# A hybrid mixer layer on one core: recurrence levels as one run of ten products, gate modulation in runs of two blocks

## The chip, the cores and the metric

The kernel runs on one core of one Trainium2 chip. The time is the device time of one execution in microseconds (us). Before the change the median of three runs is 438.06 us (437.89 to 438.6). The profile is of one more execution, which took 439.14 us.

## The reference

One layer of a diffusion backbone. 128 context tokens and 512 latent tokens of width 1024 (640 rows in all) are normalised and modulated, go through one input projection, then through three parallel mixers (attention, a gated linear recurrence in two directions, a Fourier mixing), each times a SiLU gate, and through one output projection. A second normalisation, a modulation gate and a residual add end it. Cut to what the change touches:

```python
mod = silu(c) @ w_ada + b_ada              # one vector for the context, one for the latent tokens
shift, scale, gate = split(mod, 3)         # 1024 each
h = rmsnorm(x, g_pre) * (1 + scale) + shift
proj = h @ w_in
...
# recurrence, per head (64 keys x 64 values), forward and backward over the tokens:
#   state_t = f_t * state_{t-1} + k_t v_t ,  out_t = q_t state_t
...
out = concat(attention * silu(ga), rms(recurrence) * silu(gr), fourier * silu(gf)) @ w_out
x = x + gate * rmsnorm(out, g_post)
```

The change touches two places: the recurrence inside chunks of 128 tokens, and the products silu(c) @ w_ada, in particular those for `gate`.

## The kernel before

The 640 rows lie transposed in SBUF (`hT`, a high and a low part, so that three products of the reduced type fp32r stand for one fp32 product). The input projection goes in 30 blocks of 128 columns. For each block `load_raw` (L172) brings 512 KB of weights into a tile tagged `raw`; `split_w` makes a high part by a copy on ScalarE (L127) and a low part by a subtraction on VectorE (L128), in tiles `hi` and `lo` of three buffers each; then 48 products of 320 columns follow (`block`, L295). The tag `raw` has two buffers, which the weights of the input projection (`win`), the gate (`wg`) and the output projection (`wout`) share. All weight loads go out on SyncE's queue, and `tc.issue_after(wdma[-1])` in `load_raw` keeps them in the order in which the program was written down.

That order is made by `Order` (L39): streams (generators) for the start, the recurrences of two head pairs (p = 0 and 1), the attentions, the gate vectors and the filling projection blocks are taken in turn by a rough clock of TensorE's work, and events let a stream wait for another, as `block18` for the end of the 18th projection block. The blocks are written down in the order of `FILL` (L30); blocks 18 to 26 are the second gate block of the recurrence, a gate block of attention, value, query and key of attention pair 3, two gate blocks of the Fourier mixing and its two inputs. What is written down goes through a scheduler that simulates the engines and may take a later instruction first if an earlier one isn't ready. `follow` (L115) ties a product to the one before it in a list without a semaphore, so that the two keep their order on TensorE.

**Modulation.** `mod_cols` (L192) multiplies silu of the two conditioning vectors (`csil`, 32 columns) with a block of 128 columns of w_ada, k = 0 to 7. The eight fp32 products write to four strips of 32 rows of one bank, k and k + 4 to the same strip. In `start_stream` (L242) each of eight steps does two such blocks into one bank, for scale and shift. In `gate_vectors` (L842) eight steps q each wait for `block18` to `block25`, load one block of gate weights, do one `mod_cols` into a bank of its own and split the result into two halves of `rows`; after each odd q four products with `selr` (L870) sum the strips and spread the vector over the partitions.

**Recurrence.** For each head pair p, `recurrence` (L412) builds the matrix of decayed query-key products of each 128-token unit in seven levels h = 1, 2, 4, ... 64. At each level ScalarE (L458 to L461) and VectorE (L464 to L473) prepare `QB` and `KB`. `level` (L429) then does ten fp32 products of 64 rows: five units times two heads. The heads lie in the two halves of the rows. The first eight go to two banks, the last two to two more. Then the wanted part of each bank is copied into `AL` (units 0 to 3) and `AC` (unit 4): at the first level all of it by ScalarE, at the others by `copy_predicated` on VectorE (L448) with a mask of the token pairs whose indices first differ at this level. For h = 64 that mask is the two off-diagonal quadrants of 64x64. The banks come from `PB()`, which has five buffers for its tag `b` and three for the tag `f` of the projection blocks. After the last level the diagonal is set by two more masked copies for each head (L485, L486).

Of the kernel before, what the change touches and what calls it, by code (L numbers as in the profile page):

```python
# [10 lines left out]
F32R = mybir.dt.float32r  # L11
# [6 lines left out]
P = 128  # L18
# [4 lines left out]
LEVELS = [1, 2, 4, 8, 16, 32, 64]  # L23
# [48 lines left out]
def mixer_kernel(ctx: ExitStack, tc: tile.TileContext, A, O):  # L72
    nc = tc.nc
    sc, ve, gp, te, sy = nc.scalar, nc.vector, nc.gpsimd, nc.tensor, nc.sync
# [5 lines left out]
    sp = ctx.enter_context(tc.tile_pool(name="sp", bufs=WB["s"]))  # L80
    ps = ctx.enter_context(tc.tile_pool(name="ps", bufs=8, space=PSUM))

    od = Order()
# [3 lines left out]
    def nm(s):  # L87
        n_[0] += 1
        return f"{s}_{n_[0]}"

    def T(cols=NT, dt=F32, tag=""):
        return tp.tile([P, NT], dt, tag="t", name=nm("t" + tag))[:, :cols]
# [12 lines left out]
    def PB(tag="b"):  # L105
        return ps.tile([P, 512], F32, tag=tag, name=nm("pb"), bufs=WB["p" + tag])
# [3 lines left out]
    def mm(out, lhsT, rhs, start=True, stop=True):  # L110
        n, m = rhs.free_size(), lhsT.free_size()
        od.now += 1e-3 * (n * 0.4167 * 4 if rhs.dtype == F32 else max(n * 0.4167, m * 0.83)) + 2e-3
        return te.matmul(out, lhsT, rhs, start=start, stop=stop).ins  # L113

    def follow(chain, ins):  # L115

        if chain:
            tc.add_manual_dep(ins, chain[-1].name, mybir.DependencyInfo(mybir.DependencyClass.NoSync,
                                                                        mybir.DependencyReason.DATA), reason="turns")
        chain.append(ins)  # L120
# [5 lines left out]
    def split(src, hi, lo, hi_eng=None, lo_eng=None):  # L126
        (sc.copy if hi_eng is None else hi_eng.tensor_copy)(hi, src)  # L127
        (ve if lo_eng is None else lo_eng).tensor_sub(lo, src, hi.bitcast(F32))  # L128
# [5 lines left out]
    def const(name, shape, dt=F32, dma=gp.dma_start):  # L134
        t = cp.tile([P, *shape], dt, tag=name, name=name)
        if name in A:
            dma(t, A[name])
        return t
# [6 lines left out]
    RS = [slice(0, 64), slice(64, 128)]  # L145
# [20 lines left out]
    csil = const("csil", [KT, 32])  # L166
# [5 lines left out]
    def load_raw(src, tag, shape=(KT, P)):  # L172
        t = (tp if tag == "vs" else wp).tile([P, *shape], F32, tag=tag, name=nm(tag), bufs=WB[tag])
        with tc.issue_after(wdma[-1]) if wdma else ExitStack():
            wdma.append(sy.dma_start(t, src).ins)
        return t
# [12 lines left out]
        with tc.issue_after(wdma[-1]) if wdma else ExitStack():  # L189
            sy.dma_start(t, src)  # L190

    def mod_cols(out, w):  # L192

        t = od.now
        for k in range(KT):
            o = out[32 * (k % 4):32 * (k % 4) + 32, :]
            mm(o, csil[:, k, :], w[:, k, :], start=(k < 4), stop=(k >= 4))
        od.now = t + 0.45

    shift, G, rstd = const("shift", [KT, 2]), const("G", [KT, 2]), const("rstd", [5])  # L200
# [14 lines left out]
    def load_x():  # L215
        for i in range(5):
            load(xa[i], A["x"][i * P:(i + 1) * P, 0:NT])
            load(xb[i], A["x"][i * P:(i + 1) * P, NT:D])

    def scale_x():  # L220
        for i in range(5):
            ss2 = S(2)
            sc.activation(T(), xa[i], ACT.Square, accum_out=ss2[:, 0:1])
            ve.tensor_tensor_reduce(PE_()[:, 0:384], xb[i], xb[i], 1.0, 0.0, op0=ALU.mult, op1=ALU.add,
                                    accum_out=ss2[:, 1:2])
            ve.tensor_add(rstd[:, i:i + 1], ss2[:, 0:1], ss2[:, 1:2])
            rsqrt_mean(rstd[:, i:i + 1], D)
            ve.tensor_scalar(xa[i], xa[i], rstd[:, i:i + 1], 0.0, op0=ALU.mult, op1=ALU.add)
            ve.tensor_scalar(xb[i], xb[i], rstd[:, i:i + 1], 0.0, op0=ALU.mult, op1=ALU.add)
# [12 lines left out]
    def start_stream():  # L242
        load_x()
        raws, zraw = [], []

        def loads(k):
            for u in range(2):
                raws.append(load_raw(A["wss"][2 * k + u], RAW[2 * k + u]))
            if k < 2:
                zraw.append(load_raw(A["win"][k], "raw"))  # L250

        for k in range(EARLY):
            loads(k)
        scale_x()
        od.now = 11.0
        for k in range(KT):
            if k + EARLY < KT:
                loads(k + EARLY)
            row = sp.tile([P, 256], F32, tag="AC", name=nm("row"), bufs=2)
            pm = PB()  # L260
            for u in range(2):
                mod_cols(pm[:, u * P:(u + 1) * P], raws[2 * k + u])
            yield 0
            ve.tensor_copy(row, pm[:, 0:256])
            yield LAT["row"]
            pt = pm[:, 256:260]
            for u in range(2):
                mm(pt[:, u * 2:u * 2 + 2], row[:, u * P:(u + 1) * P], sel[:, :, 0:1].rearrange("p a b -> p (a b)"))
            ve.tensor_scalar(G[:, k, :], pt[:, 0:2], bss[:, k, 0:1], 1.0, op0=ALU.add, op1=ALU.add)
            ve.tensor_scalar_mul(G[:, k, :], G[:, k, :], gpre[:, k:k + 1])  # L270
            ve.tensor_scalar_add(shift[:, k, :], pt[:, 2:4], bss[:, k, 1:2])
            modulated(k, pm)
            if k < 2:
                zf_w.append(split_w(zraw[k]))
            if k == 1:
                od.set("zw", 0.0)
            yield max(0.0, 13.5 + 2.7 * (k + 1) - od.now)
# [134 lines left out]
    def recurrence(p):  # L412
# [3 lines left out]
        q = qg[p]  # L416
# [6 lines left out]
        AL = wp.tile([P, 2, 4, P], F32, tag="pT", name=nm("AL"), bufs=WB["pT"])  # L423
        AC = sp.tile([P, 2, P], F32, tag="AC", name=nm("AC"), bufs=2)
# [4 lines left out]
        def level(KB, QB, li):  # L429


            mk = late["masks"][:, li, :].unsqueeze(1)
            for i0, i1 in ((0, 4), (4, 5)):
                pa = [PB(), PB()]
                t, chain = od.now, []
                for i in range(i0, i1):
                    for hh in (1, 0):
                        ins = mm(pa[hh][:, (i - i0) * P:(i - i0 + 1) * P], KB[RS[hh], i * P:(i + 1) * P],
                                 QB[RS[hh], i * P:(i + 1) * P])
                        follow(chain, ins)  # L440
                od.now = 0.5 * (t + od.now)
                for hh in range(2):
                    out = AL[:, hh] if i0 == 0 else AC[:, hh:hh + 1, :]
                    src = pa[hh][:, :(i1 - i0) * P].rearrange("p (a t) -> p a t", t=P)
                    if li == 0:
                        sc.copy(out, src)
                    else:
                        ve.copy_predicated(out, mk.to_broadcast([P, i1 - i0, P]), src)  # L448

        for li, h in enumerate(LEVELS):  # L450
            QB, KB = T(), T()
# [31 lines left out]
        mk = late["masks"][:, 7, :].unsqueeze(1)  # L483
# [44 lines left out]
        for i in range(5):  # L528
            o = po[i // 4][:, i % 4 * P:i % 4 * P + P]
# [312 lines left out]
    def gate_vectors():  # L842
        selr = cp.tile([P, 2, P], F32R, tag="selr", name="selr")
        gp.tensor_copy(selr, sel)
        for q in range(8):
            yield f"block{WG + q}"
            hf = q // 4
            w = load_raw(A["wg"][q], "raw")
            if q % 4 == 0:
                gbias = T(512), T(512)  # L850
                for t, name in zip(gbias, ("bgate", "gpost")):
                    load(t, A[name][hf * 512:hf * 512 + 512].partition_broadcast(P))
                if True:
                    if q == 0:
                        gc = sp.tile([P, 2, 512], F32, tag="masks", name="gc", bufs=1)
                    gg[0][hf], gg[1][hf] = gc[:, hf, :], T(512)
                else:
                    gg[0][hf], gg[1][hf] = T(512), T(512)
            if q % 2 == 0:
                rows = [sp.tile([P, 256], F32R, tag="AC", name=nm("row"), bufs=2) for _ in range(2)]  # L860
            pm, es = PB("f"), slice(q % 2 * P, q % 2 * P + P)
            mod_cols(pm[:, 0:P], w)
            split(pm[:, 0:P], *[t[:, es] for t in rows])
            if q % 2 == 0:
                continue
            yield 1.0
            pg, cs = PB("f"), slice(q % 4 * P - P, q % 4 * P + P)
            for d in range(2):
                for a in range(2):
                    mm(pg[:, d * 256:d * 256 + 256], selr[:, d, :], rows[a], start=(a == 0), stop=(a == 1))  # L870
            for d in range(2):
                g = gg[d][hf][:, cs]
                ve.tensor_add(g, pg[:, d * 256:d * 256 + 256], gbias[0][:, cs])
                ve.tensor_mul(g, g, gbias[1][:, cs])
# [254 lines left out]
```

## Time and profile before

| | |
|---|---|
| median of three runs | 438.06 us |
| the profiled execution | 439.14 us |
| its span (first to last recorded work) | 437.3 us |
| TensorE products, busy | 413.5 us |
| VectorE, busy | 302.3 us |
| ScalarE, busy | 205.1 us |
| granted TensorE clock, mean | 0.998 |

A span has 1.8 us less than the execution, since start and end of the program lie around it. A line of the profile names the engine (PE TensorE, PEld its weight loads, DVE VectorE, ACT ScalarE, SPq the queue of SyncE), the line of the code, the operation, and the tiles out<-in with their shapes. L113 is the helper `mm`, so all products carry that line, and the tiles tell them apart: `pb<-raw,csil` are the gate's modulation products, `pb<-t,t` with 64*128 those of the levels, `pb<-hT,hi` and `pb<-hT,lo` the input projection's, `tqs` and `pe` belong to attention. Rows of a timeline start with the start and the length in us; "xN" counts records, and an idle time before the instruction stands in brackets with what ended it. Rows of groups have the count, then the busy time in us and the mean in ns, then idle time before them. An engine's busy time can overlap another's, so the shares don't add up.

### The profile page before, as it was taken

How to read it: one execution, taken by the hardware profiler on the slowest of the kernel's cores; microseconds unless marked ns; L12 is line 12 of the kernel's file. 1: busy time of each engine (PE TensorE's matmuls, PEld its weight loads, DVE VectorE, ACT ScalarE, POOL GpSimd, SP SyncE). 2: the span in 40 equal slices, each digit the busy share in tenths (PEclk: the TensorE clock that was granted, in tenths of full speed). 3: DMA queues.
4: the chain of work that ended last, by engine and by line, in shares of the span. 5: the costliest groups of instructions: out<-in, count | busy, mean ns of one | idle time of the engine just before them, and what ended most of it. 6: DMA issues, size and time to landing. Idle time of an engine off the chain costs nothing.

```text
span 437.3 us, 8333 instructions
## 1 busy us (share of the span) xinstructions
PE 413.5 (95%) x3192; PEld 375.1 (86%) x3192; DVE 302.3 (69%) x858; ACT 205.1 (47%) x546; POOL 7.4 (2%) x23
## 2 busy tenths in 40 slices
PE   0699999999998999999999999999999999999994
PEld 0488999999987998999899889989898988988884
DVE  2765478999987775885497748886768928670174
ACT  5533366566341525654454544743456643250151
POOL 2000000000020100000000000000000000000000
PEclk9999999999999999999999999999999999999999
DMA  7995144121211111132112413345134302481033
GB/s 243 412 407 216 48 117 150 50 72 49 59 49 46 37 64 48 55 97 58 47 54 73 146 48 103 98 135 161 61 120 146 98 0 65 140 276 61 0 119 124
DMA packets 19528, 47.62 MB, mean 109 GB/s; under 512 B 3184, under 2 KB 6912, under 8 KB 19488
## 3 DMA queue, kind: packets, MB, share of 16 engines
q1 hardware_dynamic: 19376, 46.94, 31.7%
q8 instruction: 25, 0.41, 0.4%
q0 software_dynamic: 112, 0.14, 0.2%
q14 instruction: 15, 0.12, 0.1%
HBM read 43.80 MB, written 3.28 MB: 108 GB/s over the span
## 4 chain that ended last, share of the span: by engine, by line
PE 91%; DVE 3%; DMA 3%; ACT 1%; issue 1%; SPq 0%; DVEq 0%; ACTq 0%
PE pb L113 85%; PE pb L124 6%; DMA vs<-wss 1%; DMA txa<-x 1%; DVE AL L448 1%; DVE t L522 1%; DVE AL L485 0%; ACT L677 0%; DVE t L951 0%; ACT pe L678 0%; DVE t L465 0%; DVE t L464 0%; DVE AC L448 0%; DVE t L466 0%; SPq L190 0%
## 5 line engine op out<-in xcount | busy, mean ns | idle before, releaser
L113 PE MATMUL pb<-hT,hi 128*128 128x320 f32 x896 | 209.0, 317 | 2.5 <-DVE vs L128 1.5
L113 PEld LDWEIGHTS pb<-hT,hi 128*128 128x128 f32 x896 | 148.9, 188 | 9.0 <-issue 3.3
L113 PE MATMUL pb<-hT,lo 128*128 128x320 f32 x448 | 139.2, 312 | 0.0
L113 PEld LDWEIGHTS pb<-hT,lo 128*128 128x128 f32 x448 | 84.0, 188 | 1.3 <-issue 0.2
L128 DVE TENSOR_TENSOR lo<-raw,hi 128x1024 fp32r<-128x1024 f32 x35 | 42.8, 1222 | 21.1 <-ACT hi L127 20.7
L127 ACT CAST hi<-raw 128x1024 fp32r<-128x1024 f32 x35 | 36.8, 1050 | 29.1 <-PE pb L113 17.5
L113 PE MATMUL pb<-t,t 64*128 64x128 f32 (+2 forms) x414 | 42.9, 291 | 0.4 <-DVE AL L448 0.4
L113 PEld LDWEIGHTS pb<-t,t 64*128 64x128 f32 (+1 forms) x414 | 36.0, 188 | 4.7 <-issue 0.7
L127 ACT CAST pT<-pb 128x256 fp32r<-128x256 f32 x64 | 23.4, 372 | 23.0 <-PE pb L124 11.4
L113 PE MATMUL pb<-hi,mh 128*128 128x512 f32 (+1 forms) x108 | 30.8, 376 | 0.0
L128 DVE TENSOR_TENSOR pT<-pb,pT 128x256 fp32r<-128x256 f32 x64 | 26.4, 417 | 1.7 <-ACT pT L127 1.5
L677 ACT ACTIVATE pe<-pb,s 128x256 f32<-128x256 f32 x32 | 15.2, 476 | 17.5 <-DVE s L676 8.5
L113 PEld LDWEIGHTS pb<-hi,mh 128*128 128x128 f32 x108 | 19.7, 188 | 3.8 <-DVE mh L128 0.3
L113 PE MATMUL pb<-pT,mh 128*128 128x512 f32 (+1 forms) x102 | 21.9, 364 | 0.0
L124 PE MATMUL pb<-ident,pe 128*128 128x128 f32 x136 | 21.0, 274 | 0.5 <-ACT pe L678 0.5
L113 PEld LDWEIGHTS pb<-pT,mh 128*128 128x128 f32 x102 | 17.7, 189 | 3.1
L113 PE MATMUL pb<-lo,mh 128*128 128x512 f32 (+1 forms) x54 | 19.5, 376 | 0.0
L932 ACT ACTIVATE t<-pb 128x512 f32<-128x512 f32 (+1 forms) x11 | 6.0, 552 | 27.3 <-PE pb L113 27.3
L688 DVE TENSOR_TENSOR o<-pb,o 64x512 f32<-64x512 f32 (+1 forms) x16 | 7.8, 486 | 15.5 <-ACT o L687 15.4
L124 PEld LDWEIGHTS pb<-ident,pe 128*128 128x128 f32 x136 | 16.5, 140 | 1.7 <-ACT pe L678 0.7
L448 DVE COPY_PREDICATED AL<-masks,pb 128x512 f32<-128x512 uint32 x24 | 16.5, 741 | 1.8 <-PE pb L113 1.8
L113 PE MATMUL pb<-pT,vs 128*128 128x256 f32 (+1 forms) x96 | 17.0, 320 | 0.0
(204 smaller groups left out, 636.3 us busy)
## 6 DMA issues: line engine op xcount, KB each, us to landing
raw<-win SPq DMA_DIRECT2D x30, 512.0 KB, 3.4
pT<-wss SPq DMA_DIRECT2D x12, 512.0 KB, 10.2
raw<-wg SPq DMA_DIRECT2D x8, 512.0 KB, 3.4
raw<-wout SPq DMA_DIRECT2D x8, 512.0 KB, 3.8
t<-x SPq DMA_DIRECT2D x10, 256.0 KB, 5.6
o_y<-t SPq DMA_DIRECT2D x9, 256.0 KB, 2.0
vs<-wss SPq DMA_DIRECT2D x4, 512.0 KB, 9.2
tbl<-tbl SPq DMA_DIRECT2D x4, 512.0 KB, 3.9
```

Source lines behind the costliest of these rows:

```text
L113: return te.matmul(out, lhsT, rhs, start=start, stop=stop).ins
L124: last_tr[0] = te.transpose(out, src, ident).ins
L127: (sc.copy if hi_eng is None else hi_eng.tensor_copy)(hi, src)
L128: (ve if lo_eng is None else lo_eng).tensor_sub(lo, src, hi.bitcast(F32))
L448: ve.copy_predicated(out, mk.to_broadcast([P, i1 - i0, P]), src)
L522: ve.scalar_tensor_tensor(sall[r, cdst], sall[r, cs], Td[r, ip:ip + 1], pst[r, cdst], op0=ALU.mult, op1=ALU.add)
L677: sc.activation(pe[:, 256:512], ss[:, 256:512], ACT.Exp, bias=m[:, 1:2], accum_out=m[:, 3:4])
L688: ve.tensor_add(out, src[r, :], out)
L932: sc.activation(T(512)[:, cs], po[:, 0:cs.stop - cs.start], ACT.Square, accum_out=ssb[:, j:j + 1])
```

## The change

The diff has three parts. The ten products of a level form one chain over four banks instead of two chains over two banks each, and the copies come after all ten. At the last level (h = 64) ScalarE copies the two off-diagonal quadrants of each bank's part instead of the masked copy on VectorE. The modulation products of two blocks form one chain, both in the start stage and in the gate; in the gate, loads, bank and split of the blocks q - 1 and q are put together at the odd q, and at the even q only the two bias loads remain (q = 0 and 4).

```diff
-    def mod_cols(out, w):
+    def mod_cols(out, w, chain):
         t = od.now
         for k in range(KT):
             o = out[32 * (k % 4):32 * (k % 4) + 32, :]
-            mm(o, csil[:, k, :], w[:, k, :], start=(k < 4), stop=(k >= 4))
+            follow(chain, mm(o, csil[:, k, :], w[:, k, :], start=(k < 4), stop=(k >= 4)))
...
-            pm = PB()
+            pm, turns = PB(), []
             for u in range(2):
-                mod_cols(pm[:, u * P:(u + 1) * P], raws[2 * k + u])
+                mod_cols(pm[:, u * P:(u + 1) * P], raws[2 * k + u], turns)
...
-            for i0, i1 in ((0, 4), (4, 5)):
-                pa = [PB(), PB()]
-                t, chain = od.now, []
-                for i in range(i0, i1):
-                    for hh in (1, 0):
-                        ins = mm(pa[hh][:, (i - i0) * P:(i - i0 + 1) * P], KB[RS[hh], i * P:(i + 1) * P],
-                                 QB[RS[hh], i * P:(i + 1) * P])
-                        follow(chain, ins)
-                od.now = 0.5 * (t + od.now)
+            pa = [PB() for _ in range(4)]
+            t, chain = od.now, []
+            for i in range(5):
+                for hh in (1, 0):
+                    out = pa[i // 4 * 2 + hh][:, i % 4 * P:i % 4 * P + P]
+                    follow(chain, mm(out, KB[RS[hh], i * P:(i + 1) * P], QB[RS[hh], i * P:(i + 1) * P]))
+            od.now = 0.5 * (t + od.now)
+            for j, n in ((0, 4), (1, 1)):
                 for hh in range(2):
-                    out = AL[:, hh] if i0 == 0 else AC[:, hh:hh + 1, :]
-                    src = pa[hh][:, :(i1 - i0) * P].rearrange("p (a t) -> p a t", t=P)
+                    out = AL[:, hh] if j == 0 else AC[:, hh:hh + 1, :]
+                    src = pa[2 * j + hh][:, :n * P].rearrange("p (a t) -> p a t", t=P)
                     if li == 0:
                         sc.copy(out, src)
+                    elif li == len(LEVELS) - 1:
+                        for a, b in ((0, 1), (1, 0)):
+                            sc.copy(out[RS[a]][:, :, RS[b]], src[RS[a]][:, :, RS[b]])
                     else:
-                        ve.copy_predicated(out, mk.to_broadcast([P, i1 - i0, P]), src)
+                        ve.copy_predicated(out, mk.to_broadcast([P, n, P]), src)
...
         for q in range(8):
             yield f"block{WG + q}"
             hf = q // 4
-            w = load_raw(A["wg"][q], "raw")
+            chain = []
...
             if q % 2 == 0:
-                rows = [sp.tile([P, 256], F32R, tag="AC", name=nm("row"), bufs=2) for _ in range(2)]
-            pm, es = PB("f"), slice(q % 2 * P, q % 2 * P + P)
-            mod_cols(pm[:, 0:P], w)
-            split(pm[:, 0:P], *[t[:, es] for t in rows])
-            if q % 2 == 0:
                 continue
+
+            rows = [sp.tile([P, 256], F32R, tag="AC", name=nm("row"), bufs=2) for _ in range(2)]
+            pm = PB("f")
+            for u, ww in enumerate([load_raw(A["wg"][q - 1 + j], "raw") for j in range(2)]):
+                mod_cols(pm[:, u * P:(u + 1) * P], ww, chain)
+            split(pm[:, 0:256], *rows)
             yield 1.0
```

## The prediction

> **What bounds the kernel now.** I read the page's parts 1 and 4 first, then the busy time by stage, then TensorE's own timeline at the places that the diff touches, and last the queue of SyncE, which issues the weight loads.
>
> ```profile
> PE 413.5 (95%) x3192; PEld 375.1 (86%) x3192; DVE 302.3 (69%) x858; ACT 205.1 (47%) x546; POOL 7.4 (2%) x23
> PE 91%; DVE 3%; DMA 3%; ACT 1%; issue 1%; SPq 0%; DVEq 0%; ACTq 0%
> 75.90:122.00 46.10, 46.10 (x438) 42.89 (x439) 44.48 (x111) 24.95 (x61) 0.00 (x0) 1.00 0.21 64
> 122.00:136.00 14.00, 12.18 (x109) 10.72 (x108) 13.17 (x41) 6.22 (x16) 2.42 (x6) 1.00 0.05 11
> 240.00:340.00 100.00, 100.00 (x797) 89.60 (x796) 73.97 (x245) 52.16 (x164) 0.00 (x0) 1.00 0.36 113
> ```
>
> The first line is busy time by engine, the second the chain of waits, the others are stretches with the busy time of PE, PEld, DVE, ACT and POOL in that order. TensorE is the bound: 91% of the chain. In 75.9 to 122 us, where the recurrence levels run, VectorE is busy for 44.48 of 46.10 us, but TensorE never stands, because projection products fill it. In 122 to 136 us VectorE is the late one and TensorE stands for 1.82 us. In 240 to 340 us, where the gate's modulation products run, TensorE is full. So a product saved there is worth its full time, and a wait that is put there costs its full time. That second half decides this case.
>
> **The modulation products (gain).** In this trace one fp32 product leaves two records (the 64 products of the gate are 128 records), so x16 is one block of eight.
>
> ```profile
> 31.43 0.64 PE L113 MATMUL pb<-vs,csil 128*32 128x128 f32 x16
> 31.89 0.62 PE L113 MATMUL pb<-pT,csil 128*32 128x128 f32 x16
> 32.44 0.77 PE L124 MATMUL pb<-ident,txa 128*128 128x128 f32 x5
> ```
>
> The first column is the start, so a piece costs the distance to the next start. Here, at the start of the kernel, two blocks stand back to back and take 31.43 to 32.44 = 1.01 us. In the gate, block 0 is broken:
>
> ```profile
> 246.97 0.42 PE L113 MATMUL pb<-raw,csil 128*32 128x128 f32 x6
> 247.32 0.66 PE L124 MATMUL pb<-ident,pe 128*128 128x128 f32 x4
> 247.91 0.62 PE L113 MATMUL pb<-raw,csil 128*32 128x128 f32 x10
> 248.47 0.56 PE L113 MATMUL pb<-hT,hi 128*128 128x320 f32 x2
> ```
>
> That is three and five products, which take 0.35 and 0.56 us. Over the eight gate blocks I count 13 pieces: three, like this one, in two pieces each, one in three (1.04 us), four whole at 0.57 or 0.58. Together they take 6.1 us. Four unbroken pairs take 4.04, so the bare gain is 2.0 us. Each visit also costs about 0.19 us to leave and rejoin the 320-column products; the rows of the next fence show it at a level (a step of 0.147 us each, two products from 75.57 to 75.86, and the run starts only at 75.96; about as much again behind it). Chaining only orders the products among themselves; work with an earlier place can still slip in. If the breaks stay, the pairs save 4 x 0.15 us and four visits, 1.4 us; with neither it is 0.6. Unbroken it is 2.8. I take 1.8, between the two. In the start stage the blocks already run whole and in order: nothing. The merged split (one 256-column cast and subtraction instead of two of 128) saves a few tenths on ACT and DVE, off the path.
>
> **The levels (gain).** A level of ten products is x20.
>
> ```profile
> 75.43 0.31 PE L113 MATMUL pb<-hT,lo 128*128 128x320 f32 x1
> 75.57 0.46 PE L113 MATMUL pb<-hT,hi 128*128 128x320 f32 x2
> 75.96 1.39 PE L113 MATMUL pb<-t,t 64*128 64x128 f32 x20
> 77.27 0.42 PE L113 MATMUL pb<-hT,lo 128*128 128x320 f32 x1
> ```
>
> Most of the 14 levels are one run like this, 75.96 to 77.27 = 1.31 us. Two are broken. The first of them begins so:
>
> ```profile
> 79.37 0.48 PE L113 MATMUL pb<-t,t 64*128 64x128 f32 x2
> 79.79 0.56 PE L113 MATMUL pb<-hT,hi 128*128 128x320 f32 x2
> ```
>
> It is broken 1+9 (0.42 us for the lone product, and 0.19 for its visit, 0.61 extra; the nine take as long as ten). The other, early in the second half of the levels' time, is broken 1+8+1; two lone products at 0.6 us extra each, less the fifth of the run that the eight don't take, are about 1.0. So whole runs can save at most 1.6 us. A run now asks for four of the five banks before it is whole, so it may still break; the other end is 0. I take 0.8. The two halves' copies keep their order, so nothing else of the level moves. Should a run wait for its banks, the projection products, which have banks of their own, cover it at no cost, as they do at 75.9 to 122 us; without that cover each wait would cost about the copies' 2.1 us (below).
>
> **The last level's copies (gain).** They leave VectorE and go to ScalarE.
>
> ```profile
> L448 DVE COPY_PREDICATED AL<-masks,pb 128x512 f32<-128x512 uint32 x24 | 16.5, 741 | 1.8 <-PE pb L113 1.8
> L448 DVE COPY_PREDICATED AC<-masks,pb 128x128 f32<-128x128 uint32 x24 | 6.1, 299 | 0.0
> L687 ACT COPY o<-pb 64x512 f32<-64x512 f32 x8 | 4.6, 580 | 7.6 <-PE pb L113 7.4
> L687 ACT COPY o<-pb 64x128 f32<-64x128 f32 x8 | 2.1, 260 | 4.2 <-PE pb L113 4.1
> ```
>
> The first two rows are means over all levels but the first (741 and 299 ns), the others ScalarE's nearest copies. What stands idle around the last level shows here:
>
> ```profile
> 124.44 1.07 ACT L498 COPY t<-pb 128x512 f32<-128x512 f32 x2 [7.19 <-PE pb L124]
> 135.70 0.53 PE L113 MATMUL pb<-hT,hi 128*128 128x320 f32 x2 [1.46 <-DVE vs L128]
> ```
>
> VectorE loses 2 x 0.741 + 2 x 0.299 = 2.1 us per recurrence. ScalarE gets eight quadrant copies: four of 64x256, which I put at 0.37 (between the 0.260 and 0.580 of the two 64-row copies), and four of 64x64 at 0.21, together about 2.3 us. It stood idle for 7.19 us before 124.44, so this is free there. VectorE's chain up to 135.6 gets shorter, and TensorE's 1.46 us wait at 135.70 and the rest of the 1.82 us can go: at most 1.8 us. Against it: the diagonal's copy on VectorE must now wait for all eight copies of ScalarE, 2.3 instead of 2.1 us, and what is queued behind it on VectorE (the other recurrence's decay products, and the split named in the last row) stands with it; if it also pays two hand-overs that may be 0.6 us lost. I take a gain of 1.0. What is late next is then TensorE itself.
>
> **The loads of the gate's weights (loss).** This is the term I believe largest. The raw weights, the gate's and the projection's alike, share two buffers and one queue in program order.
>
> ```profile
> SPq L175 <- PE pb L113: 44.7, 10, 9.3
> ```
>
> This row is from the waits of that queue: ten times weight loads stood for products, 44.7 us in all. Now the queue itself in order of time:
>
> ```profile
> 228.52 0.33 SPq L175 DMA_DIRECT2D raw<-wg  x1
> ...
> 248.56 0.33 SPq L175 DMA_DIRECT2D raw<-win  x1
> 254.31 0.33 SPq L175 DMA_DIRECT2D raw<-wg  x1
> ...
> 309.88 0.33 SPq L175 DMA_DIRECT2D raw<-win  x1
> 316.34 0.33 SPq L175 DMA_DIRECT2D raw<-wg  x1
> ```
>
> And TensorE at the second gate block:
>
> ```profile
> 260.81 0.62 PE L113 MATMUL pb<-raw,csil 128*32 128x128 f32 x10
> 261.37 0.50 PE L113 MATMUL pb<-kc,tqs 64*128 64x256 f32 x4
> ...
> 263.55 0.42 PE L113 MATMUL pb<-raw,csil 128*32 128x128 f32 x6
> 263.90 0.56 PE L113 MATMUL pb<-hT,hi 128*128 128x320 f32 x2
> ```
>
> Gate block 1 is loaded at 228.52, and its products start only at 260.81, at the end of projection block 19, while block 0's stand at the end of block 18. All eight stand at their projection block's end in this way, however early their data came. A gate load therefore holds its buffer until then, and only then does the next projection load go out: at 248.56, 0.09 us after block 0's products have ended at 248.47. Today that is harmless, since gate and projection loads alternate: while one buffer waits for the gate's products, the other passes projection weights. The weights loaded at 248.56 are first used at 263.90.
>
> The change puts the loads of q-1 and q together, at the end of the projection block of the odd q, and it moves the load of q-1 behind one projection load. The queue becomes win 19, wg 0, wg 1, win 20, win 21, wg 2, wg 3 and so on. Both buffers then hold gate weights at the end of block 19, and the weights of block 20, which TensorE wants next, can't start to load before the first eight products of the pair have run. The same holds at blocks 22, 24 and 26: four times. From a projection load's issue to its weights being cast and split took 248.56 to 254.31 = 5.75 us here (the split's end frees the buffer, and the next gate load goes out); over the six such pairs (the first and the last are shown) it is 5.75 to 7.31, mean 6.45. With 0.1 us to issue, less the 0.55 us of the pair's second half, 6.0 us are uncovered. Cover is what attention has ready: 261.37 to 263.55 = 2.2 us at the first place. So a stall lies between 0 (all covered) and 3.8 us. I take 2.75: the 2.2 us seen and about 1 us more, since a TensorE that stands will be given attention work of later places. Four stalls are 11.0 us, between 0 and 15.
>
> **The sum.** The profiled execution took 439.14 us, 437.3 of span and 1.8 around it. 439.14 - 1.8 - 0.8 - 1.0 + 11.0 = 446.5. It lies 1.08 above the median of 438.06, so against the median I forecast 445.5.
>
> **Rivals.** First, the stalls are hidden. If attention (or a scheduler that places the pair's products earlier) covers all 6.0 us, only the gains stay: 439.14 - 3.6 - 1.08 = 434.5. It turns at a cover of about 5.1 us per place, where 4 x 0.9 equals the 3.6 gained. For it: the pair's data land long before block 19 ends, and an earlier place would free the buffers in time. Against it: none of the eight blocks moved up today, and attention shows 2.2 us of ready work, not 5.1. Second, no change: the runs stay as broken as they are and the loads are hidden, 437.2 to 438.9. Third, the standing array runs slow afterwards:
>
> ```profile
> 14.21 1.08 PE L113 MATMUL pb<-vs,csil 128*32 128x128 f32 x16 [14.21 <-DMA vs<-wss]
> ...
> 23.10 0.64 PE L113 MATMUL pb<-vs,csil 128*32 128x128 f32 x16
> ```
>
> After the first 14.21 us without work a run of eight takes 1.08 us, and 0.64 from 23.10 on; right behind the 1.46 us at 135.70 two products take 0.53, like the 0.56 behind an ordinary change of work. A stall of 2.75 us lies between. If each were followed by such a stretch, at most 8.9 us at 0.59 of the speed, that is up to 3.6 us more per stall, 14.6 in all: 460, and half of it 453. [...]
>
> **Chances and range.** About 0.9 us, 0.2%, is what can be told from no change. The forecast, stalls of 1 to 4 us each (439 to 452), has 0.62; slow stretches behind the stalls (452 to 460) 0.10; the hidden stalls with gains (432 to 437) 0.20; no change 0.08. So faster 0.20, same 0.08, slower 0.72. The range goes from 434, which takes in the middle of the faster case, to 455; the likeliest case alone is 440 to 451.
>
> **What would show it.** Right: on SyncE's queue two gate loads in a row, then a projection load straight behind the pair's first eight products; idle TensorE of 2 to 4 us at four places, ended by the cast or the split of raw weights, between 255 and 350 us; TensorE's share below 95%. The gains: pairs as x32 taking about 1.0 us, levels as x20, no wait at 135.7. Wrong: 240 to 350 us without idle TensorE, or the pair's products well ahead of their projection block's end. If the span grows by another road (waits for banks in 76 to 147 us, or slower products), my loss term had the wrong cause.

## The result, and the profile after

The changed kernel takes 451.06 us (median of five runs, 449.59 to 451.77) beside 438.6 us for the kernel before (five runs of the same session, 437.89 to 438.76). The ratio is 1.0284, interval 1.0263 to 1.0305: slower by about 12.5 us. The profiled execution took 451.06 us as well, 448.9 of it span; before it was 439.14 with 437.3, so 11.6 us of span are to be explained. The mean granted clock fell from 0.998 to 0.988.

From the page of the changed kernel, busy time by engine and the chain by engine:

```profile
PE 416.4 (93%) x3192; PEld 378.9 (84%) x3192; DVE 299.3 (67%) x846; ACT 209.3 (47%) x558; POOL 7.6 (2%) x23
PE 85%; DVE 5%; DMA 4%; ACT 3%; issue 1%; SPq 0%; DVEq 0%; ACTq 0%
```

The number of products is the same, 3192 records, yet PE is busy for 2.9 us more, and its share of the chain fell from 91% to 85%. So there is new idle time, and some products have become slower. The two stretches of the prediction and the one around the last levels, in the changed kernel (busy time of PE, PEld, DVE, ACT and POOL, then granted clock, DMA share, GB/s):

```profile
122.00:136.00 14.00, 11.93 (x104) 10.48 (x102) 11.73 (x37) 8.36 (x24) 2.65 (x6) 1.00 0.05 11
122.00:160.00 38.00, 35.01 (x293) 32.57 (x291) 27.39 (x78) 18.31 (x52) 4.57 (x12) 1.00 0.14 40
240.00:340.00 100.00, 94.73 (x716) 86.58 (x714) 67.32 (x225) 45.97 (x150) 0.00 (x0) 0.97 0.29 90
```

240 to 340 us was full and now holds 5.27 us without work, at a clock of 0.97. In 122 to 136 us VectorE has 1.44 us less to do than before (11.73 for 13.17), but TensorE stands a little longer (2.07 us for 1.82). SyncE's queue of the changed kernel, in order of time (x2 and x3 merge issues):

```profile
223.26 0.33 SPq L175 DMA_DIRECT2D raw<-wg  x1
...
229.67 0.33 SPq L175 DMA_DIRECT2D raw<-wg  x1
...
261.02 2.67 SPq L175 DMA_DIRECT2D raw<-win  x2
267.69 3.67 SPq L175 DMA_DIRECT2D raw<-wg  x2
...
286.07 2.12 SPq L175 DMA_DIRECT2D raw<-win  x2
...
315.06 0.33 SPq L175 DMA_DIRECT2D raw<-win  x1
...
341.67 6.24 SPq L175 DMA_DIRECT2D raw<-win  x3
```

The order is the one forecast: two gate loads in a row, both buffers held, and the next projection load only when the pair's first eight products are through. TensorE of the changed kernel at the second of the four places (start, length, and in brackets the idle time before and what ended it):

```profile
285.37 0.85 PE L113 MATMUL pb<-raw,csil 128*32 128x128 f32 x20
...
291.07 0.87 PE L113 MATMUL pb<-hT,hi 128*128 128x320 f32 x2 [2.12 <-ACT hi L127]
...
293.13 0.47 PE L113 MATMUL pb<-hT,lo 128*128 128x320 f32 x1
293.39 0.73 PE L113 MATMUL pb<-hT,hi 128*128 128x320 f32 x2
```

The projection load goes out at 286.07 and its first products start at 291.07, 5.00 us later. Work covers 2.88 us of that, and TensorE stands for 2.12, until the cast of the raw weights. What follows is slow: the 320-column product at 293.13 holds the array for 0.26 us (to 293.39) instead of the 0.147 of before. The other three places, from the same view of the changed kernel:

```profile
264.94 0.66 PE L124 MATMUL pb<-ident,t 128*128 128x128 f32 x4 [0.37 <-DVE o L690]
265.54 0.56 PE L113 MATMUL pb<-hT,hi 128*128 128x320 f32 x2
...
267.72 0.42 PE L113 MATMUL pb<-hT,lo 128*128 128x320 f32 x1 [0.85 <-DVE lo L128]
...
319.79 0.56 PE L113 MATMUL pb<-hT,hi 128*128 128x320 f32 x2 [1.13 <-ACT hi L127]
...
321.91 0.64 PE L113 MATMUL pb<-hT,lo 128*128 128x320 f32 x1 [0.80 <-DVE lo L128]
...
346.36 0.56 PE L113 MATMUL pb<-hT,hi 128*128 128x320 f32 x2 [1.51 <-ACT hi L127]
```

All but one of these waits end at the cast or the split of raw weights; the first, of 0.37 us, ends at an output of attention. The four places together stand for 1.22 + 2.12 + 1.93 + 1.51 = 6.78 us.

The levels, in the changed kernel (the broken one of the first recurrence, then the broken one of the second):

```profile
78.94 0.48 PE L113 MATMUL pb<-t,t 64*128 64x128 f32 x2
...
80.28 1.38 PE L113 MATMUL pb<-t,t 64*128 64x128 f32 x18
...
130.32 0.48 PE L113 MATMUL pb<-t,t 64*128 64x128 f32 x2
...
131.52 1.16 PE L113 MATMUL pb<-t,t 64*128 64x128 f32 x16
...
135.51 0.53 PE L113 MATMUL pb<-hT,hi 128*128 128x320 f32 x2 [1.47 <-DVE vs L128]
...
138.32 0.48 PE L113 MATMUL pb<-t,t 64*128 64x128 f32 x2
```

The level that was broken 1+9 is still broken 1+9, the other is still 1+8+1, and the wait of 1.46 us is still there, as 1.47.

My account of the 11.6 us of span, from the two traces: +6.78 idle behind the pairs; +3.4 from a halved clock in two stretches of 3.41 us (the last section shows them); +1.16 more idle time in 122 to 160 us (2.99 for 1.83); -0.44 from the modulation products (ten pieces of 5.64 us in all for thirteen of 6.08). That is 10.9; the other 0.7 I can't place. Two differences lie outside these places: the stretch behind the start of TensorE's last product is 0.7 us longer (441.78 to 448.9, before 430.91 to 437.3), and the first level starts 0.4 us earlier (75.53 for 75.96).

### The profile page after: what moved, and what is told of

Its sections match the earlier page's. It is cut to its first block, busy times and chain, and to the rows that moved or that the text cites. A ratio compares the mean times of both kernels' runs of the same rounds, so it can differ in the third digit from the quotient of the medians.

```text
span 448.9 us, 8339 instructions
## 1 busy us (share of the span) xinstructions
PE 416.4 (93%) x3192; PEld 378.9 (84%) x3192; DVE 299.3 (67%) x846; ACT 209.3 (47%) x558; POOL 7.6 (2%) x23
## 4 chain that ended last, share of the span: by engine, by line
PE 85%; DVE 5%; DMA 4%; ACT 3%; issue 1%; SPq 0%; DVEq 0%; ACTq 0%
PE pb L113 80%; PE pb L124 5%; DMA raw<-win 2%; DMA vs<-wss 1%; DMA txa<-x 1%; DVE t L524 1%; DVE s L675 1%; DVE lo L128 1%; ACT AL L448 0%; ACT hi L127 0%; ACT AC L448 0%; DVE m L676 0%; ACT t L500 0%; ACT L679 0%; ACT L161 0%
## 5 line engine op out<-in xcount | busy, mean ns | idle before, releaser
L113 PEld LDWEIGHTS pb<-hT,hi 128*128 128x128 f32 x896 | 150.9, 190 | 12.5 <-ACT hi L127 5.4
L680 ACT ACTIVATE pe<-m,s 128x256 f32<-128x256 f32 x32 | 16.2, 506 | 0.0
```

The lines of the kernel that those rows point to most:

```text
L680: sc.activation(pe[:, 0:256], sb, ACT.Exp, bias=m[:, 1:2], accum_out=m[:, 2:3])
```

## The experiments

Theory A is the prediction's, corrected by what the trace shows: the pair holds both raw buffers, TensorE stands four times behind it, and the clock adds to the cost; the last level's copies cost a little, the levels nothing. The main rivals are these: the copies or the levels carry much of the loss; the order of the queue, not the holding of buffers, is what counts; the slow stretches belong to the pairs' products and not to the standing. All ratios are against the kernel before, in the same session.

**The three parts, one at a time.** Each starts from the kernel before and takes over one part of the change. Levels alone:

```diff
-            for i0, i1 in ((0, 4), (4, 5)):
-                pa = [PB(), PB()]
+            pa = [PB() for _ in range(4)]
...
+            for i in range(5):
+                for hh in (1, 0):
+                    out = pa[i // 4 * 2 + hh][:, i % 4 * P:i % 4 * P + P]
+                    follow(chain, mm(out, KB[RS[hh], i * P:(i + 1) * P], QB[RS[hh], i * P:(i + 1) * P]))
```

> The kernel before with one part of the change alone: the ten products of a level as one chain over four banks, copies as they were. Theory A (in the changed kernel's profile the levels stand in the same pieces as before: one 1+9, one 1+8+1, the rest whole): the chain changes nothing, ratio 1.000, within 0.1%. Rival (the term of the prediction): up to 1.6 us of broken runs go, 0.8 us or 0.2% faster. Rival C: a run that asks for four banks at once costs, then it is slower by some tenths of a per cent, with idle time of TensorE between 76 and 147 us above the 1.8 us of before.

Measured: 438.87 us, ratio 1.0004 (0.9994 to 1.0015). No effect.

Last level's copies alone:

```diff
+                    elif li == len(LEVELS) - 1:
+                        for a, b in ((0, 1), (1, 0)):
+                            sc.copy(out[RS[a]][:, :, RS[b]], src[RS[a]][:, :, RS[b]])
```

> The kernel before with the last level's copies alone moved from VectorE (masked) to ScalarE (quadrants). Theory A (from the changed profile, where TensorE stood 3.0 us between 122 and 160 us instead of 1.8): 1.0 to 1.2 us slower, 0.25%, with TensorE's extra idle time before the transposes of the second recurrence, whose bank is held until ScalarE has done its copies behind a square root with its table load. Rival (the prediction): 1.0 us faster, the 1.46 us wait near 135.7 us gone.

Measured: 440.21 us, ratio 1.0034 (1.0020 to 1.0048): a loss of about 1.5 us, where I had forecast a gain of 1.0.

The modulation runs of two blocks alone (in the start stage as in the change, and in the gate; the gate's part is shown):

```diff
-            w = load_raw(A["wg"][q], "raw")
+            chain = []
...
-            mod_cols(pm[:, 0:P], w)
-            split(pm[:, 0:P], *[t[:, es] for t in rows])
+            for u, ww in enumerate([load_raw(A["wg"][q - 1 + j], "raw") for j in range(2)]):
+                mod_cols(pm[:, u * P:(u + 1) * P], ww, chain)
+            split(pm[:, 0:256], *rows)
```

> The kernel before with the gate's and the start stage's modulation runs alone changed; levels and their copies as before. Theory A: nearly all of the loss is here, 10 to 11 us slower than before (ratio about 1.025), with TensorE idle for 6 to 7 us at four places behind the pairs and two stretches of about 3.4 us with the granted clock at 0.5 (about 3.4 us more). Rival: the loss is spread over the parts or comes from their meeting, then this is under 7 us.

Measured: 448.3 us, ratio 1.0220 (1.0193 to 1.0247), a loss of 9.7 us. The three parts alone add up to 0.2 + 1.5 + 9.7 = 11.4 of the 12.5 us; the other 1.1 lie within the interval of the third. The profiled execution is the slowest of four (450.67 us). TensorE of this kernel at its third and fourth place, and the stretch that was full before:

```profile
319.31 0.90 PE L113 MATMUL pb<-hT,hi 128*128 128x320 f32 x2 [1.13 <-ACT hi L127]
...
344.58 0.56 PE L113 MATMUL pb<-hT,hi 128*128 128x320 f32 x2 [1.17 <-ACT hi L127]
```

```profile
240.00:340.00 100.00, 95.27 (x730) 86.73 (x730) 67.57 (x227) 46.95 (x153) 0.00 (x0) 0.97 0.29 90
```

TensorE stands at the same four places, 5.90 us in all for the changed kernel's 6.78. All but the first wait (0.37 us) end at a cast or split of raw weights again. The gate part holds the loss of the second half.

**Queue order or held buffers.** In the changed kernel each gate block is loaded at its own turn again, so that a projection load goes between the two, while the products stay in pairs:

```diff
+            wq = [wq[1] if q else None, load_raw(A["wg"][q], "raw")]
...
-            for u, ww in enumerate([load_raw(A["wg"][q - 1 + j], "raw") for j in range(2)]):
+            for u, ww in enumerate(wq):
```

> The changed kernel, but each gate block is loaded at its own q, as before the change, and only the products wait for the pair. It tells the order of the loads from the holding of the buffers. Theory A (two buffers hold two gate blocks until the pair's products have run, wherever in the queue they were loaded): no better than the changed kernel, 449 to 452 us, the same four idle places ended by the cast or split of raw weights. Rival (the two gate loads in a row push the projection load back in the queue): it comes back to 439 to 441 us.

Measured: 450.91 us, ratio 1.0278 (1.0243 to 1.0313), the same as the changed kernel. SyncE's queue of this kernel, then TensorE at its fourth place:

```profile
222.89 0.33 SPq L175 DMA_DIRECT2D raw<-win  x1
...
229.30 0.33 SPq L175 DMA_DIRECT2D raw<-wg  x1
...
260.65 0.33 SPq L175 DMA_DIRECT2D raw<-win  x1
```

```profile
347.72 0.56 PE L113 MATMUL pb<-hT,hi 128*128 128x320 f32 x2 [2.33 <-ACT hi L127]
```

The loads alternate again, and the projection load still waits from 229.30 to 260.65 for a buffer. So it isn't the order: two buffers that wait for the same late products leave none, in whichever order they were filled. One thing came out otherwise than expected: at the second and third place the waits end at attention's softmax (1.20, 1.53, 1.72 and 0.37 us), not at a cast or a split. The weights aren't there by then either; at the second place their cast ends only at 292.98, behind both waits.

**A third raw buffer.** Room for it comes from two other tags, and the same edit was put on the changed kernel, on the kernel before (control), and on the gate part alone:

```diff
-WB = {"raw": 2, ..., "t": 18, ..., "cf": 3, ...}
+WB = {"raw": 3, ..., "t": 17, ..., "cf": 2, ...}
```

> The changed kernel with a third buffer for raw weights. To make room, the tag t has 17 buffers instead of 18 and cf two instead of three. Theory A (the loss is the buffers that the pair holds): the four idle places and the half clock behind them go, 439 to 441 us, of which about 1.2 us belong to the last level's copies. Rival (the loss is the pair's long run or the transfer itself): it stays above 447 us. A third outcome, about 445, would say that one buffer more only shortens the stalls, or that the smaller tags cost something, which the next kernel shows.

> The kernel before with the same buffers as e5 (raw 3, t 17, cf 2): the control. Theory A: before the change weights came in time with two buffers (TensorE full from 240 to 340 us), so the third brings nothing, 438 to 440 us, and any difference is the price of the smaller tags. Rival: it is over 1 us faster than before, then e5's gain isn't due to the pair alone.

> The modulation runs of two blocks without the rest of the change, with the buffers of e5 (raw 3, t 17, cf 2). Theory A: with the stalls gone the pairs' gain shows, and the copies of the last level cost nothing: 437.5 to 439 us, about 1.2 us below e5, at or a little below the kernel before. Rival: as e5, then the last level's copies are not what e5 pays.

Measured: the changed kernel 443.08 us (1.0096, 1.0076 to 1.0116); the kernel before 439.98 (1.0027, 1.0016 to 1.0039); the gate part 442.13 (1.0079, 1.0064 to 1.0095). The stretch 240 to 340 us of the changed kernel with three buffers:

```profile
240.00:340.00 100.00, 100.00 (x793) 90.39 (x792) 72.32 (x237) 50.55 (x160) 0.00 (x0) 1.00 0.36 116
```

It is full again, at full clock. That is the causal test of the main term: one more buffer takes away the standing and the slow stretches with it, some 8 us. But both kernels with the pairs came out above what I expected. The smaller tags cost the control 1.25 us, and the first kernel, which has the levels and the last level's copies too, is 0.95 us slower than the third. That leaves 2.15 us by which the gate part, with nothing standing behind its pairs, is still slower than its control. The pairs bring no gain even then: the modulation products take 6.03 us in ten pieces, those of the control 5.60 in eleven. These 0.43 us explain a fifth of it. In the two profiles the first level starts 1.24 us later with the pairs (75.81 for 74.57 us). But the changed kernel and three of its variants, whose code is the same up to there, start it anywhere from 75.14 to 76.63, so one execution each can't settle this, and the cause of the rest stays open.

**Filling the idle time.** Behind each pair twelve 256-column products go to a bank whose content is overwritten later; their results are unused, and they add work. The second form puts them at the second place alone:

```diff
+            pg, cs = PB("f"), slice(q % 4 * P - P, q % 4 * P + P)
+            t = od.now
+            for _ in range(12):
+                mm(pg[:, 0:256], hT[0][:, 0, 0:P], hT[0][:, 0, 0:256])
+            od.now = t
```

```diff
+            for _ in range(12 if q == 3 else 0):
```

> The changed kernel with 12 extra products of 256 columns behind each pair, into the bank that the gate's next products overwrite; their results are not used. They are about 12 x 0.12 = 1.4 us of work per pair, 5.8 us in all, laid into places where TensorE stood 1.2, 2.1, 1.9 and 1.5 us. Theory A (the idle time also costs by the clock that is halved behind it, 1.7 us each behind the second and third place): the work replaces idle time, the granted clock stays at 1.00, and the kernel gets faster by up to 3.4 us, 447 to 449.5 us. Rival (the halved clock isn't due to the idle time): no change or slower by the part of the work that finds no idle time, 451 to 453 us, with the clock halved as before.

> The changed kernel with the 12 extra products of e7 behind the second pair alone (q = 3), where TensorE stood longest, 2.1 us, and the granted clock fell to 0.5 behind it; their results are not used. In e7 the clock stayed at 1.00 there, but the extra products put the third place's attention out of step. Theory A (the idle time costs itself and, by the clock, 1.7 us more): the extra 1.4 us of work stands in idle time, the clock stays at 1.00 at this place, and the kernel is 0.5 to 2 us faster than the changed one, 449 to 450.5 us. Rival (the clock falls for another reason, or the work only pushes the rest): the same or slower, 451 to 453 us.

Measured: at all four places 452.5 us (1.0315, 1.0271 to 1.0359), no faster than the changed kernel; at the second place alone 448.49 (1.0219, 1.0194 to 1.0244), 2.6 us below the changed kernel's median though it has about 1.4 us more to compute. The kernel with the filler at one place, around the place where the changed kernel stood:

```profile
292.00:294.00 2.00, 2.00 (x15) 2.00 (x15) 1.82 (x5) 2.00 (x6) 0.00 (x0) 1.00 0.79 266
```

TensorE doesn't stand at this place any more, and the clock is 1.00 in 292 to 294 us, where the changed kernel had 0.50. The pair's products are all still there, so they alone don't bring the slow stretch. But standing alone doesn't bring it each time either. The third place of the same execution, which has no filler, and the clock in the stretch with its stalls and in the one behind:

```profile
317.87 0.56 PE L113 MATMUL pb<-hT,hi 128*128 128x320 f32 x2 [1.13 <-ACT hi L127]
...
320.00 0.41 PE L113 MATMUL pb<-hT,lo 128*128 128x320 f32 x1 [0.80 <-DVE lo L128]
```

```profile
315.81:319.23 3.42, 2.25 (x20) 1.77 (x19) 3.33 (x12) 2.89 (x7) 0.00 (x0) 1.00 0.60 193
319.23:322.64 3.41, 2.64 (x18) 2.65 (x19) 3.41 (x11) 2.00 (x5) 0.00 (x0) 1.00 0.42 153
```

TensorE stands 1.13 and 0.80 us there, as in the changed kernel, yet the clock stays at 1.00. So of the 3.7 us between the two spans (448.9 and 445.2) about 1.7 (half of 3.41) belong to a slow stretch at a place that the filler doesn't touch, and this execution alone doesn't show that the filler kept the clock up at the second place. Nor do the five executions, two of which seem to have a slow stretch somewhere: three with a mean clock of 0.997 took 446.82 to 448.49 us, the two with 0.991 and 0.992 took 448.76 and 450.42.

With the filler at all places it went otherwise, at the third one above all (TensorE of that kernel):

```profile
322.87 0.63 PE L124 MATMUL pb<-ident,pe 128*128 128x128 f32 x4 [1.33 <-DVE pe L683]
```

There TensorE waits 1.33 us for attention's `pe`, then 1.30 for the weights, and the clock is at half for 6.8 us (0.50 in every 1 us from 325 to 331 us). That the extra products held attention up is my reading of the order; it wasn't tried. The time lies in the rival's range, so this run is nothing for the theory; since new waits came in, it isn't a clean test against it either.

**One pair alone.** On the kernel before, only blocks 2 and 3 become a pair:

```diff
-            w = load_raw(A["wg"][q], "raw")
+            if q not in (2, 3):
+                w = load_raw(A["wg"][q], "raw")
...
+            if q == 3:
+                chain = []
+                for u, ww in enumerate([load_raw(A["wg"][2 + j], "raw") for j in range(2)]):
+                    mod_cols(pm[:, u * P:(u + 1) * P], ww, chain)
+                split(pm[:, 0:256], *rows)
```

> The kernel before with only the blocks q = 2 and 3 loaded and multiplied as a pair, the other six as before. Theory A (each place pays for itself): TensorE stands about 2.1 us behind this pair and nowhere else between 240 and 350 us, and the clock falls to half for about 3.4 us behind it, 1.7 us lost: 3.3 to 4.2 us slower than before, 442 to 443 us. Rival (the stalls add up only when four follow each other, or the neighbours' loads give the time back): under 2 us slower.

Measured: 441.51 us, ratio 1.0065 (1.0042 to 1.0087), a loss of 2.9 us, a little under the range expected. TensorE of this kernel at the place, and its busy time and clock behind it:

```profile
289.82 0.56 PE L113 MATMUL pb<-hT,hi 128*128 128x320 f32 x2 [1.78 <-ACT hi L127]
```

```profile
292.00:294.00 2.00, 2.00 (x10) 2.00 (x9) 1.85 (x11) 1.66 (x8) 0.00 (x0) 0.50 0.83 281
```

The profiled execution is the slowest of six (443.57 us); its span is 4.5 us longer than that of the kernel before (441.8 for 437.3). Of these, 1.78 are standing, 1.7 a half clock for 3.41 us, and 1.1 a later start of the first level (77.08 for 75.96). The six executions fall into two groups: three with a mean clock of 0.999 took 439.71 to 440.77 us, three with 0.992 to 0.995 took 442.25 to 443.57. The middle ones lie 2.05 and 3.70 us above the kernel before, close to the standing alone (1.78) and to the standing with one slow stretch (3.5). So one pair is enough for the whole mechanism, without the other three, and the slow stretch comes in some executions and not in others. The other three places weren't run alone.

**Which recurrence's last level.** The copies on ScalarE for one of the two recurrences only, on the kernel before:

```diff
+                    elif li == len(LEVELS) - 1 and p == 0:
+                        for a, b in ((0, 1), (1, 0)):
+                            sc.copy(out[RS[a]][:, :, RS[b]], src[RS[a]][:, :, RS[b]])
```

and with `p == 1` in the second kernel.

> As e2, the last level's copies on ScalarE, but only in the first recurrence (p = 0). Theory A (the price is the second recurrence's copies, which ScalarE does in two parts around a square root with its table load, while the banks are held): nearly nothing here, 0 to 0.4 us slower than before. Rival (ScalarE's copies and their hand-over to VectorE cost the same in both): half of e2's 1.5 us, 0.75 us.

> As e2, but only in the second recurrence (p = 1). Theory A: nearly all of e2's price, 0.9 to 1.3 us slower than before, with TensorE idle near 148 us. Rival: 0.75 us, as in e10.

Measured: the first recurrence 438.9 us (1.0005, 0.9994 to 1.0016), nothing; the second 440.04 (1.0034, 1.0022 to 1.0047), the whole loss of the copies. ScalarE at that place, first in the kernel before, then in the changed one:

```profile
144.38 1.28 ACT L161 ACT_TABLE_LOAD   x1
...
147.12 1.07 ACT L498 COPY t<-pb 128x512 f32<-128x512 f32 x2 [1.15 <-PE pb L124]
```

```profile
144.23 1.52 ACT L448 COPY AL<-pb 64x256 f32<-64x256 f32 x4
145.76 1.28 ACT L161 ACT_TABLE_LOAD   x1
147.06 0.30 ACT L161 ACTIVATE s<-s,eps 128x10 f32<-128x10 f32 x1
147.39 0.88 ACT L448 COPY AC<-pb 64x64 f32<-64x64 f32 x4
148.29 1.07 ACT L500 COPY t<-pb 128x512 f32<-128x512 f32 x2
```

Before, ScalarE loaded a table and took a square root in time that it had to spare, and still waited 1.15 us for TensorE. Now the load and the root stand between the two halves of the copies, and the copy that the next step needs begins at 148.29 instead of 147.12. TensorE of the kernel with the second recurrence's copies alone shows who pays:

```profile
147.67 0.66 PE L124 MATMUL pb<-ident,t 128*128 128x128 f32 x4 [0.52 <-ACT AC L449]
148.72 1.49 PE L113 MATMUL pb<-t,t 128*128 128x128 f32 x11 [0.40 <-ACT t L501]
```

0.92 us of the 1.5 are these two waits. That the table load is what makes them is read from the queue; the copies without the load between them weren't run.

## Why the prediction was right or wrong

The forecast was 445.5 us, slower, with 434 to 455; it came out at 451.06, slower. The direction and its main cause were right, and the size is made of errors of both signs: the standing came out smaller than forecast, all the other terms went upward.

- **The loads of the gate's weights.** Right in the mechanism, in the queue's order and in the four places; one more buffer removes it. The size of the standing was forecast too high, 11.0 us for 6.78. The step that failed is "6.0 us are uncovered" with 3.25 of cover. From the issue of the projection load to its first products it was 4.52, 5.00, 4.73 and 4.69 us at the four places (the first is 261.02 to 265.54) and not the 6.45 behind the 6.0, since the first products need only the cast, and I had counted to the end of the split. Work covered 4.15, 2.88, 3.60 and 3.18 us of that, the pair's second half included: mean 3.45, a little less than the 3.8 assumed (3.25 and 0.55). At the first and third place a second wait, for the split, adds 0.85 and 0.80.
- **The third rival, slow products behind the stalls,** was right in kind and came on top, where I gave it a chance of 0.10: 3.4 us in the profiled execution. I took it for unlikely because behind the 1.46 us wait at 135.70 the products had run at full speed. That row was no guide for the other places, as the last section shows. By their mean clocks, other executions of the same kernel had less or more of it. No run shows the 452 us where I let its range begin; the profiled execution, with two slow stretches of 1.7 us each, took 451.06.
- **The last level's copies.** Wrong in sign: +1.0 of gain forecast, 1.5 us of loss measured. The step that failed is "so this is free there". I read ScalarE's 7.19 us of idle time before 124.44, in the first recurrence's last level, and took it for the second one too, where the table load and the root are queued. The hoped-for end of the wait at 135.70 failed as well: VectorE does 1.44 us less in that stretch and the wait is as long as before, so its amount of work isn't what sets the wait. What does, wasn't found.
- **The levels.** 0.8 of gain forecast, none measured. The prediction's lower end was right: the chain orders the ten products, and other work still slips in at the same two levels. Why just there wasn't tried.
- **The modulation products.** 1.8 of gain forecast; the pieces save 0.44 us. Pairs are broken into 9+7, 10+6, 3+9+4 and 9+3+4, so most visits remain. With three buffers, where nothing stands behind the pairs, there is no gain either.

Set against the sum of 446.5, the profiled 451.06 is 4.6 us higher: the standing takes 4.2 away; the clock adds 3.4, the copies 2.2 (1.0 of gain missed and 1.16 of new idle time), the gate runs 1.4, the levels 0.8, what I can't place 0.7, and the time around the span 0.3. The error of 5.6 against the median would have been near 10 without the first term's excess, so that the size came this near is in part luck.

## What to carry to other kernels

Before two consumers are joined, ask which buffers their operands hold until then, and who takes the next one: with two buffers in a shared tag, the pair that was consumed late stopped the tag's other loads here, from 229.67 to 261.02 us in the changed kernel and from 229.30 to 260.65 with the loads in the other order. The same step on another engine cost nothing in the first recurrence (438.9 us), where that engine had 7.19 us to spare, and 1.4 us in the second, where a table load of 1.28 us stands in its queue; so read the queue at every place where the step will stand. An order between products isn't a contiguous run: if the gain rests on their being together, look in the trace whether anything slipped in.

## What the runs showed of the hardware

Between 240 us and its last product the changed kernel's granted TensorE clock fell to 0.50 twice. Four narrow windows hold the edges of these slow stretches (the clock is the third number from the right):

```profile
291.00:291.25 0.25, 0.18 (x1) 0.18 (x2) 0.20 (x1) 0.25 (x2) 0.00 (x0) 0.75 0.84 262
294.50:294.75 0.25, 0.25 (x3) 0.25 (x3) 0.25 (x2) 0.25 (x2) 0.00 (x0) 0.92 0.57 213
321.75:322.00 0.25, 0.09 (x1) 0.09 (x1) 0.25 (x2) 0.25 (x1) 0.00 (x0) 0.69 0.00 0
325.25:325.50 0.25, 0.25 (x3) 0.25 (x3) 0.25 (x3) 0.00 (x0) 0.00 (x0) 0.98 0.11 16
```

Between the edges the clock reads 0.50 (291.13 to 294.54 and 321.85 to 325.26), in front of them and behind them 1.00. So a mean of 0.75 over 291.00 to 291.25 puts the fall at 291.13; the other edges lie at 294.54, 321.85 and 325.26 in the same way. Both stretches last 3.41 us, and they start 30.72 us apart, near 9 x 3.41. In the kernel with the gate part alone there are three of this length, from 291.96, 319.26 and 346.57, twice 27.31 us apart, near 8 x 3.41. No run shows where these distances come from.

The falls came with short stalls: behind 240 us the longest between products is 2.12 us in the changed kernel and 2.39 us in the one with the gate part alone. In the changed kernel, the 3.41 us in front of the first fall, and 3.41 us that brought no fall:

```profile
287.72:291.13 3.41, 1.29 (x10) 0.99 (x10) 2.54 (x10) 1.90 (x4) 0.00 (x0) 1.00 0.80 246
...
134.12:137.53 3.41, 2.02 (x14) 2.05 (x15) 3.25 (x9) 0.86 (x1) 0.00 (x0) 1.00 0.00 0
```

2.12 us of idle time stand in front of the first fall, and in the gate part alone 1.08 and 1.16 us in the 3.41 us in front of 319.26 and 346.57. Yet 1.39 us at 134 us brought no fall, nor did the 1.51 us stall that ends at 346.36 (the clock of the changed kernel reads 1.00 from 326 to 444 us). So the amount of idle time alone doesn't tell them apart. The 3.41 us at 134 us held nothing but the projection's 320-column products, while those in front of a fall also held shorter and narrower ones, scores and transposes among them. That doesn't tell them apart either: in the kernel with the filler at the second place, 315.81 to 319.23 held 1.17 us of idle time and attention's scores (its row stands with that experiment), and the clock reads 1.00 from 240 to 360 us. What brings a fall stays open.

In these kernels a stall of one or two microseconds cost 1.7 us more (half of 3.41), or not: the same two stalls at the third place, 1.13 and 0.80 us, came with a slow stretch in the changed kernel and without one in the kernel with the filler. One such stretch lowers the mean clock of 449 us by 0.004 (3.41 x 0.5 / 449). The five executions of the changed kernel fit: 449.59 us at 0.992, 450.56 and 451.06 at 0.989 and 0.988, 451.67 and 451.77 at 0.985. So their spread of 2.2 us, for 0.9 before, goes with the slow stretches, though only the profiled one, at 0.988, is shown to have two.
